# The S5 parameters prepared anew: fused on VectorE, padded on ScalarE, loaded by GpSimd, and the S5 scans joined

## The chip, the cores and the metric

One core of one Trainium2 chip runs the whole kernel. The number reported is device time in microseconds of that core, as the median of several runs. The engines are TensorE (PE; its weight loads are PEld), VectorE (DVE), ScalarE (ACT), GpSimd (POOL) and SyncE (SP, which here only issues DMAs). Each engine takes its instructions in the order in which they were written for it, and waits at an instruction until everything that it depends on is there.

## The reference

Two layers of three sublayers each on 256 tokens of width 1024, all in float32. Each sublayer ends in `h = LN(alpha h + f(h))`.

```
sublayer 0, 2, 3, 5:  f = 0.5 * (silu(h W_gate) * (h W_up)) W_out        # width 2816
sublayer 1 (S5):      u = h W_in                                         # 64 groups of 16 channels, 64 complex states each
    dt = exp(log_dt); lam = exp(a dt)         # a = a_re + i a_im
    Bbar = (lam - 1) / a * B
    state[t] = lam state[t-1] + Bbar u[t]     # forward scan over 256 tokens
    y = gelu(Re(C state) + d u);  f = (y * sigmoid(y W_glu + b)) W_out
sublayer 4 (gMLP):    u, v = split(gelu(h W_in + b)); v = LN(v)
    f = (u * (mask(W_s) v + b_s)) W_out       # token mixing in blocks of 128
```

## The kernel before, in words

**Precision.** Matmuls run in float32r. Each operand is split into two parts, `hi` (the rounded value) and `lo` (the rest), and each product is three matmuls: hi hi, hi lo, lo hi.

**Weights.** `Stream` holds all weights as blocks of 1 MiB in the order of their use. SP loads a block into one of three buffers (`raw`), ACT casts it to `hi` (L82), DVE subtracts to get `lo` (L83). At most five split blocks exist at a time, those in use counted; this is the ring. `tick()` (L116) is called after every piece of PE's work: it splits one more block if the ring has room and then runs one entry of `ws.background`, a list of work that has nothing to do with the sublayer that is running.

**The first FFN (sublayer 0).** Its width is cut into 11 chunks of 256 columns. `chunk_in(c)` multiplies a chunk for all tokens in two halves m, each a gate part and an up part, and `act_t` (L364) makes silu(gate) * up on ACT and DVE and writes it, split again, into a buffer `gt` (seven exist). Its order is silu (ACT), product `sgg` (DVE), cast `gt` (ACT), difference `gt` (DVE). Beside chunk c the output product of chunk c - 2 runs in two steps, `step_out(c - 2, 0)` and `(…, 1)`, one for each half of the tokens. So chunk 0 has 3 ticks, chunk 1 has 4 and each later chunk 6 (chunk 10 has no output steps and 4 ticks). `close` does the last three output blocks, and the norm of each half of the tokens, and starts the next sublayer's transposes (`make_xt`, L177).

**The preparation.** `prepare_s5` (L577) turns the S5 parameters into the layouts of their use while the first FFN runs. Its pieces are entries of `ws.background`. A hand-written table (L878 to L907) gives each tick one piece for POOL (`work_p`) and pieces for DVE and ACT (`work_v`):

- `exp`, `angle`, `sines`, `lambdas`, `coefs`: dt, lam, lam^4 and the coefficients of Bbar. Everything is 128 x 32 (state x pair of groups), real and imaginary parts in tiles of their own, on POOL. `spread` copies the coefficients into another layout (16 copies, POOL).
- `seed`, `base_table`, `table`: cosines and sines of k times the angle of lam^4, grown by doubling; one `table` for each of eight groups of 128 channels (`ct`), two levels each, on POOL. Every second `table` writes into a buffer of the tag `gt`.
- `b_rows` and `b_turn`: Bbar lam^d in rows, transposed on DVE, written to DRAM (`rows`) by SP.
- `c_load`, `c_turn`, `c_lam`: C is loaded into a cleared tile where the two groups of a pair stand apart (half of it zeros), transposed, and multiplied by lam three times: once on DVE, twice on POOL.
- `b_bar` and `k_products`: short products K on PE. They need Bbar and C lam^d, zero where the groups differ (`bar`, `c`); `k_products(0)` and `(2)` stand at entries 58 and 59 of the table.

The results go to DRAM (`rows`, `tc`, `res["k"]`) and come back in the S5 sublayer. All loads of the preparation are issued by SP, between those of the weights.

**The S5 loop (`s5`, L910).** For each of eight `ct`: `inject` (PE), `turned` (DVE, two instructions: times cosines and sines), `sums` (POOL, two), `scan` (DVE, eight scans over 64 steps: two parts x four pairs), `turned` and `sums` again, `read_out` (PE), `activate` (DVE, ACT), `split_y` (POOL). Between them DVE splits the weights of the gate and PE multiplies with them.

Of the kernel before, what the change touches and what calls it, by code (L numbers as in the profile page):

```python
# [38 lines left out]
N_SMALL = 18  # L39


class Stream:
# [94 lines left out]
def hybrid(ctx: ExitStack, tc: tile.TileContext, a: dict, out: bass.AP, subs=SUBS):  # L137
# [137 lines left out]
    def plan_ffn(li, fi, fine):  # L275
# [31 lines left out]
    def ffn(ids, li, si, first, last):  # L307
# [132 lines left out]
    def close_mixer(ids, li, si, operand, gb, hscale, eps, last):  # L440
        """The output product of a mixer; operand(k, t): the two parts of 128 of its columns, transposed."""
# [18 lines left out]
    def load_gmlp(pool):  # L460
        """The parameters of the gMLP mixer but for its two projections; W_s masked and transposed."""
# [24 lines left out]
    def gmlp(plan, par, pool, li, si, first, last):  # L486
# [20 lines left out]
        def step_u(hd):  # L507
            """u of one head, its channels on the partitions."""
# [19 lines left out]
        def spatial(hd):  # L528
            """The token mixing of two heads and the gate, in place of u."""
# [35 lines left out]
    def load_column(pool, src, name):  # L565
        """[1024] as [128, 8], channel 128 j + p at [p, j]."""
# [10 lines left out]
    def prepare_s5(sm, qp, dram):  # L577
        """Parameters of the S5 mixer in the layouts of its use, as pieces of work for the time of the first FFN.

        State s of pair q is state s % 64 of group 2 q + s // 64. Four tokens make one step:  # L580
        S' = lam^4 S + sum over t of lam^(3-t) B u[4k+t], y[4k+3] = Re(C S'), and for t < 3
        y[4k+t] = Re(C lam^(t+1) S) + sum over i <= t of K(t-i) u[4k+i], K(d) = Re(C lam^d B).
        With lam^4 = m e^(i phi), e^(-i phi k) S is a scan with real factors m.
        """
        V, G = nc.vector, nc.gpsimd
        MUL, ADD, SUB = ALU.mult, ALU.add, ALU.subtract
        small = lambda name: sm.tile([P, PAIRS], F32, tag="sm", name=name, bufs=N_SMALL)
# [3 lines left out]
        def tt(e, o, x, y, op):  # L591
            e.tensor_tensor(o, x, y, op=op)  # L592
# [6 lines left out]
        load = nc.sync.dma_start  # L599
        m4 = sm.tile([P, PAIRS], F32, name="m4")  # L600
        val, zs = {}, []
        res = {"m4": m4, "rows": dram.tile([CT, P, 2, 4, P], F32, name="rows"), "tc": dram.tile([CT, P, D], F32, name="tc")}

        def loads():
            x = val["raw"] = big("s5a", [PAIRS, 4, P])
            for j, nm in enumerate(("s5_a_re", "s5_a_im")):
                load(out=x[:, j], in_=a[nm][0].rearrange("(q g) p -> q (g p)", g=2))
            val["dt2"] = sm.tile([PAIRS, 2], F32, name="dt2")
            load(out=val["dt2"], in_=a["s5_log_dt"][0].rearrange("(q g) -> q g", g=2))
            for j, nm in enumerate(("s5_d", "s5_b_glu")):  # L610
                load(out=x[CT * j:CT * j + CT, 3], in_=a[nm][0].rearrange("(j p) -> j p", p=P))

        def exp(x, name):
            """e^x: 2^k of the nearest integer k to x / ln 2, in two factors, times a polynomial in the rest."""
            k, r, o = small("ek"), small("er"), small(name)
            e = [small("ee") for _ in range(2)]
            ts(G, x, x, -170.0, ALU.max, 170.0, ALU.min)
            ts(G, k, x, 1.0 / math.log(2.0), MUL, ROUND, ADD)
            ts(G, k, k, -ROUND, ADD, 1.0, MUL)
            ts(G, r, k, -LN2[0], MUL, 0.0, ADD)  # L620
            tt(G, r, x, r, ADD)
            ts(G, o, k, -LN2[1], MUL, 0.0, ADD)
            tt(G, r, r, o, ADD)
            ts(G, o, r, 1.0 / 5040.0, MUL, 1.0 / 720.0, ADD)
            for n in (120.0, 24.0, 6.0, 2.0, 1.0, 1.0):
                tt(G, o, o, r, MUL)
                ts(G, o, o, 1.0 / n, ADD, 1.0, MUL)
            ts(G, r, k, -126.0, ALU.max, 127.0, ALU.min)
            tt(G, k, k, r, SUB)
            for j, part in enumerate((r, k)):  # L630
                ts(G, e[j], part, 127.0, ADD, ROUND, ADD)
            val[name], val["e"] = o, e

        def exp_end(name):
            for e in val["e"]:
                V.tensor_scalar(e.bitcast(I32), e.bitcast(I32), 23, None, op0=ALU.logical_shift_left)
                tt(G, val[name], val[name], e, MUL)

        def turn_a():
            x = val["raw"]  # L640
            G.tensor_copy(x[:, 2].rearrange("q (g p) -> q g p", g=2), over(val["dt2"], 64))
# [4 lines left out]
            for j, nm in enumerate(("ar", "ai", "ldt")):  # L646
                val[nm] = small(nm)
                nc.scalar.copy(val[nm], ps[:, PAIRS * j:PAIRS * j + PAIRS])
            dg = sm.tile([P, 2 * CT], F32, name="dg")
            res["d"], res["bg"] = dg[:, 0:CT], dg[:, CT:2 * CT]  # L650
            nc.scalar.copy(dg, ps[:, 3 * PAIRS:3 * PAIRS + 2 * CT])
            exp(val["ldt"], "dt")

        def angle():
            exp_end("dt")
            th, n, x = tt(G, small("th"), val["ai"], val["dt"], MUL), small("n"), small("x")
            ts(G, n, th, 1.0 / (2.0 * math.pi), MUL, ROUND, ADD)
            ts(G, n, n, -ROUND, ADD, 1.0, MUL)
            for part in TWO_PI:
                ts(G, x, n, -part, MUL, 0.0, ADD)  # L660
                tt(G, th, th, x, ADD)
            ts(G, th, th, 3.1415925, ALU.min, -3.1415925, ALU.max)
            val["th"] = th

        def magnitude():
            exp(tt(G, small("adr"), val["ar"], val["dt"], MUL), "mag")

        def sines():
            cs, sn = small("cs"), small("sn")
            nc.scalar.activation(cs, val["th"], AF.Sin, scale=0.5)  # L670
            nc.scalar.activation(sn, val["th"], AF.Sin)
            val["cs"], val["sn"] = cs, sn
            exp_end("mag")

        def lambdas():
            cs, sn, mag, ar, ai = (val[x] for x in ("cs", "sn", "mag", "ar", "ai"))
            tt(G, cs, cs, cs, MUL)
            ts(G, cs, cs, -2.0, MUL, 1.0, ADD)
            lr, li, den, t1 = small("lr"), small("li"), small("den"), small("t1")
            tt(G, m4, mag, mag, MUL)  # L680
            tt(G, m4, m4, m4, MUL)
            tt(G, lr, mag, cs, MUL)
            tt(G, li, mag, sn, MUL)
            tt(G, den, ar, ar, MUL)
            tt(G, t1, ai, ai, MUL)
            tt(G, den, den, t1, ADD)
            val.update(lr=lr, li=li, den=den)
# [513 lines left out]
```

## Time and profile before

| | |
|---|---|
| runs | 1043.42, 1044.12, 1046.18 us; median 1044.12 |
| profiled execution | span 1044.0 us, the only time that it has |
| busy, share of the span | PE 92%, DVE 62%, ACT 40%, POOL 29% |
| mean granted clock of TensorE | 0.964 |
| DMA | 194.86 MB, mean 187 GB/s |

A row of the timeline has its start and duration in us, the engine, line and operation, `out<-in`, the shape, and in brackets the idle time before it with what ended it. A row of groups has a count, the busy time, and the mean duration in ns. A row of windows has PE, PEld, DVE, ACT and POOL busy time in the stretch, PE's granted clock, the DMA engines' busy share and GB/s. The row of a source line has minimum, median and maximum in ns.

### The profile page before, as it was taken

The numbers are of one execution on the slowest core, as the hardware profiler recorded it, in microseconds if no ns is written. First come the engines' busy times: TensorE is split into PE (matmuls) and PEld (weight loads), VectorE is DVE, ScalarE is ACT, GpSimd is POOL, SyncE is SP. The second block draws the span as 40 slices with busy tenths as digits, with TensorE's granted clock in tenths as the row PEclk, the third lists the DMA queues.
The fourth block names the chain that finished last, engine by engine and source line by source line (L and its number), as shares of the span: only waits on it lengthen the run. The fifth ranks groups of instructions, "written<-read, shape, count | busy, mean of one in ns | idle before, by whom it ended". The sixth has DMA issues, their size and how long they took to land.

```text
span 1044.0 us, 16750 instructions
## 1 busy us (share of the span) xinstructions
PE 964.5 (92%) x6988; PEld 871.9 (84%) x6988; DVE 651.6 (62%) x726; ACT 413.1 (40%) x467; POOL 302.0 (29%) x461
## 2 busy tenths in 40 slices
PE   7999974577988889999999999999999999999996
PEld 6999963475877678999999799999978979999995
DVE  5659834588489776654536764545388785545444
ACT  5462333232143244453533363534335535443430
POOL 1589999998156421000000400000031030000001
PEclk9999996697998999999999999999999999999999
DMA  9977553385466434746455667465544565546431
GB/s 282 205 216 236 184 150 126 130 298 180 169 216 239 149 127 161 258 147 216 164 200 178 223 209 258 149 215 170 193 162 174 190 209 194 204 160 221 142 122 41
DMA packets 146124, 194.86 MB, mean 187 GB/s; under 512 B 26992, under 2 KB 117184, under 8 KB 146048
## 3 DMA queue, kind: packets, MB, share of 16 engines
q1 hardware_dynamic: 142304, 180.81, 52.7%
q0 software_dynamic: 3456, 12.45, 3.5%
q8 instruction: 55, 0.90, 0.3%
q10 hardware_dynamic: 288, 0.52, 0.1%
q14 instruction: 21, 0.17, 0.0%
HBM read 183.94 MB, written 9.83 MB: 186 GB/s over the span
## 4 chain that ended last, share of the span: by engine, by line
PE 59%; POOL 20%; DVE 10%; issue 4%; ACT 3%; DMA 2%; SPq 1%; POOLq 0%; DVEq 0%; ACTq 0%
PE ips L192 10%; PE ips L191 10%; PE ips L190 10%; PE acc L183 5%; PE acc L184 5%; PE acc L185 5%; POOL rot L972 3%; DVE lo L83 2%; POOL fac L592 2%; POOL t L592 2%; PE ips L185 2%; POOL cl L592 2%; PE ips L183 2%; PE ips L184 2%; POOL tb L592 2%
## 5 line engine op out<-in xcount | busy, mean ns | idle before, releaser
L83 DVE TENSOR_TENSOR lo<-raw,hi 128x2048 fp32r<-128x2048 f32 (+1 forms) x146 | 333.9, 2318 | 85.2 <-ACT hi L82 82.5
L190 PE MATMUL ips<-xt,hi 128*128 128x256 f32 x1184 | 335.3, 283 | 0.0
L191 PE MATMUL ips<-xt,hi 128*128 128x256 f32 x1184 | 335.0, 283 | 0.0
L192 PE MATMUL ips<-xt,lo 128*128 128x256 f32 x1184 | 335.0, 283 | 0.0
L82 ACT CAST hi<-raw 128x2048 fp32r<-128x2048 f32 (+1 forms) x156 | 275.1, 1797 | 62.7 <-PE acc L185 22.1
L190 PEld LDWEIGHTS ips<-xt,hi 128*128 128x128 f32 x1184 | 227.1, 192 | 1.4
L191 PEld LDWEIGHTS ips<-xt,hi 128*128 128x128 f32 x1184 | 227.2, 192 | 1.4
L192 PEld LDWEIGHTS ips<-xt,lo 128*128 128x128 f32 x1184 | 227.1, 192 | 0.0
L203 POOL TENSOR_SCALAR rstd<-mv 128x1 f32<-128x1 f32 x14 | 10.3, 733 | 586.3 <-DVE mv L224 564.4
L183 PE MATMUL acc<-hi,gt 128*128 128x512 f32 x352 | 141.9, 403 | 29.3 <-ACT hi L82 29.3
L184 PE MATMUL acc<-lo,gt 128*128 128x512 f32 x352 | 141.2, 401 | 4.6 <-DVE lo L83 4.6
L185 PE MATMUL acc<-hi,gt 128*128 128x512 f32 x352 | 140.2, 398 | 0.0
L369 DVE TENSOR_TENSOR sgg<-ips,sgg 128x256 f32<-128x256 f32 x74 | 31.1, 420 | 158.8 <-ACT sgg L368 158.8
L368 ACT ACTIVATE sgg<-ips 128x256 f32<-128x256 f32 x74 | 28.4, 383 | 207.9 <-PE ips L192 204.0
L183 PEld LDWEIGHTS acc<-hi,gt 128*128 128x128 f32 x352 | 68.5, 195 | 43.2 <-ACT hi L82 29.7
L370 ACT CAST gt<-sgg 128x256 fp32r<-128x256 f32 x74 | 30.1, 406 | 149.9 <-DVE sgg L369 100.9
L184 PEld LDWEIGHTS acc<-lo,gt 128*128 128x128 f32 x352 | 68.3, 194 | 18.8 <-DVE lo L83 5.9
L185 PEld LDWEIGHTS acc<-hi,gt 128*128 128x128 f32 x352 | 68.1, 193 | 14.7
L371 DVE TENSOR_TENSOR gt<-sgg,gt 128x256 fp32r<-128x256 f32 x74 | 34.1, 461 | 69.9 <-ACT gt L370 69.9
L183 PE MATMUL ips<-hi,xt 128*128 128x512 f32 x112 | 45.9, 410 | 1.7 <-ACT hi L92 1.0
L972 POOL TENSOR_TENSOR rot<-rot 128x256 f32<-128x256 f32 x32 | 35.8, 1137 | 40.1 <-DVE rot L966 39.8
L185 PE MATMUL ips<-hi,xt 128*128 128x512 f32 x112 | 45.0, 402 | 0.1
(250 smaller groups left out, 1275.9 us busy)
## 6 DMA issues: line engine op xcount, KB each, us to landing
raw<-in_ffn_w_in SPq DMA_DIRECT2D x172, 512.0 KB, 5.5
raw<-in_ffn_w_out SPq DMA_DIRECT2D x44, 1024.0 KB, 5.1
raw<-in_g_w_in SPq DMA_DIRECT2D x8, 1024.0 KB, 5.9
rows<-w SPq DMA_DIRECT2D x8, 512.0 KB, 6.0
raw<-in_s_w_in SPq DMA_DIRECT2D x4, 1024.0 KB, 5.5
raw<-in_s_w_glu SPq DMA_DIRECT2D x4, 1024.0 KB, 5.0
w<-rows SPq DMA_DIRECT2D x8, 512.0 KB, 5.8
tc<-tc SPq DMA_DIRECT2D x8, 512.0 KB, 5.1
```

The lines of the kernel that those rows point to most:

```text
L82: nc.scalar.copy(hi[:, s], raw[:, s])
L83: eng[p % len(eng)].tensor_tensor(lo[:, s], raw[:, s], hi[:, s].bitcast(F32), op=ALU.subtract)
L183: nc.tensor.matmul(ps, xh, wh, start=start, stop=False)
L184: nc.tensor.matmul(ps, xh, wl, start=False, stop=False)
L185: nc.tensor.matmul(ps, xl, wh, start=False, stop=stop)
L190: nc.tensor.matmul(ps, wh, xh, start=start, stop=False)
L191: nc.tensor.matmul(ps, wh, xl, start=False, stop=False)
L192: nc.tensor.matmul(ps, wl, xh, start=False, stop=stop)
L369: nc.vector.tensor_tensor(g, ps[:, 1], sg, op=ALU.mult)
L371: nc.vector.tensor_tensor(x[:, 1], g, x[:, 0].bitcast(F32), op=ALU.subtract)
L592: e.tensor_tensor(o, x, y, op=op)
L972: G.tensor_tensor(dst[:, j], x, z, op=ops[j])
```

## The change

`prepare_s5` is written anew, and `s5` gets new scans. The other functions are unchanged but for their docstrings and for `load_ln`, which in the first FFN now goes through POOL as in the others.

- Real and imaginary parts lie in one tile (128 x 2 x 32), and complex operations are fused: `exp` is 18 instructions (scalar_tensor_tensor), `angle` 7, `lambdas` 10, `coefs` 25, all on DVE. `seed` and `base_table` stay on POOL. `spread` goes to ACT.
- `table` goes to DVE, for two `ct` at a time, in buffers of the preparation's own; a copy of the base on ACT comes first.
- C and B are kept compact (16 columns for each pair, not 32 with zeros). `product` makes one complex part in three DVE instructions on 128 x 512, and `pad` spreads the result into the zero-padded tile with two ACT copies of 64 x 512. `c_lam` for powers 2 and 3 is made from C directly with lam^2 and lam^3, in two tiles `cl` that both powers use.
- All DMAs of the preparation are issued by POOL (60 in all), and the tiles are cleared by POOL.
- The table of entries is replaced by one list with costs. Each tick adds 1.3 us of credit (at most 1.95 is kept), and runs pieces from the head of the list while the credit is above zero or the piece costs nothing; a piece also has a first tick.
- `scan` runs over four pairs at once: the factors lie in a tile `fm` of 128 x 4 x 64, zero at the first step of each pair, filled by ACT (`factors`).

```diff
-                gb = load_ln(li, si, nc.sync if first else nc.gpsimd)
+                gb = load_ln(li, si, nc.gpsimd)
 ...
+        def cmul(o, x, y):
+            p, q = both("p"), both("q")
+            tt(p, x, twice(y[:, 0]), MUL)
+            tt(q, x, twice(y[:, 1]), MUL)
+            tt(o[:, 0], p[:, 0], q[:, 1], SUB)
+            tt(o[:, 1], p[:, 1], q[:, 0], ADD)
 ...
+        def spread(t):
+            for sq in range(4):
+                A.copy(val["cq"][32 * t:32 * t + 32, :, :, sq], val["cf"][t][32 * sq:32 * sq + 32])
 ...
+        def table(r, level):
+            q = slice(8 * r, 8 * r + 8)
             if level == 4:
-                if ct % 2:
-                    val["tb"] = gt_p.tile([P, 2, 4, NS], F32, tag="gt", name="tb")
+                val["tb"] = big("tb", [P, 2, 8, NS])
+                A.copy(val["tb"][:, :, :, 0:16], val["base"][:, :, q])
+            L, z, tb = 1 << level, val["zs"][level + 2], val["tb"]
+            x = ln_p.tile([P, 2, 2, 8, 32], F32, tag="r", name="tx", bufs=2)[:, :, :, :, 0:L]
+            for j in range(2):
+                tt(x[:, j], tb[:, :, :, 0:L], twice(over(z[:, j, q], L)), MUL)
+            tt(tb[:, 0, :, L:2 * L], x[:, 0, 0], x[:, 1, 1], SUB)
+            tt(tb[:, 1, :, L:2 * L], x[:, 0, 1], x[:, 1, 0], ADD)
 ...
+        def pad(dst, src):
             for g in range(2):
                 s = slice(64 * g, 64 * g + 64)
+                A.copy(dst[s, :, g], src[s])
+
+        def product(j, x, y, dst, signs):
+            pq = big("pq", [P, 2, PAIRS, 16])
+            tt(pq[:, 0], x[:, j], over(y[:, 0], 16), MUL)
+            tt(pq[:, 1], x[:, 1 - j], over(y[:, 1], 16), MUL)
+            tt(pq[:, 0], pq[:, 0], pq[:, 1], signs[j])
+            pad(dst, pq[:, 0])
 ...
+        def c_turn():
+            cc = val["cc"] = big("cc", [P, 2, PAIRS, 16])
+            V.transpose(cc.rearrange("p j q c -> p (j q c)"), val["cz"].rearrange("p j r c -> p (j r c)"))
+            A.mul(cc[:, 1], cc[:, 1], -1.0)
+            for j in range(2):
+                pad(val["c", 0, j], cc[:, j])
 ...
+        add(4, 0.1, turn_a)
+        add(5, 2.4, lambda: exp(val["ldt"], "dt"))
+        add(6, 1.0, angle)
+        add(7, 2.4, lambda: exp(val["ad"][:, 0], "mag"))
+        add(8, 1.3, c_turn)
+        add(9, 1.3, lambdas)
+        add(10, 0, seed, 0)
+        add(10, 3.0, coefs)
+        for t in range(T):
+            add(11, 0, spread, t)
+        for i, (f, *args) in enumerate([(b_bar, 0), (b_bar, 1), (c_lam, 1, 0), (c_lam, 1, 1), (k_products, 0), (c_lam, 2, 0),
+                                        (c_lam, 2, 1), (k_products, 2), (c_lam, 3, 0), (c_lam, 3, 1)]):
+            add(12, 0 if f is k_products else 1.8, f, *args)
+            if i < 6:
+                add(12, 0, seed, i + 1)
+        for level in range(4):
+            add(20 + level, 0, base_table, level)
 ...
+        for r in range(4):
+            for level in (4, 5):
+                add(25, (1.1, 1.9)[level - 4], table, r, level)
 ...
+        for part in range(4):
+            for j in range(2):
+                add(30, 1.9, b_rows, j, part)
+                add(30, 1.3, b_turn, j, part)
 ...
+        def tick():
+            credit[0] = min(credit[0] + PREP_US, 1.5 * PREP_US)
+            while work and work[0][0] <= ticks[0] and (credit[0] > 0.0 or work[0][1] == 0):
+                _, cost, f = work.pop(0)
+                credit[0] -= cost
+                f()
+            ticks[0] += 1
+            if work:
+                ws.background.insert(0, tick)
 ...
+        def factors(ct):
+            m = res["m4"][:, 4 * ct:4 * ct + 4].unsqueeze(2).broadcast_to([P, 4, NS - 1])
+            nc.scalar.copy(fm[ct % 2][:, :, 1:NS], m)
 ...
         def scan(ct):
+            f = fm[ct % 2].rearrange("p q k -> p (q k)")
             for j in range(2):
-                for q in range(4):
-                    f = res["m4"][:, 4 * ct + q:4 * ct + q + 1].broadcast_to([P, NS])
-                    V.tensor_tensor_scan(buf["s"][:, j, q], f, buf["v"][:, j, q], 0.0, op0=MUL, op1=ADD)
+                x, z = (buf[n][:, j].rearrange("p q k -> p (q k)") for n in "sv")
+                V.tensor_tensor_scan(x, f, z, 0.0, op0=MUL, op1=ADD)
```

More of the change, by code (lines that the diff above doesn't have):

```diff
@@ L645, in turn_a @@
             nc.tensor.transpose(ps[:, 3 * PAIRS:3 * PAIRS + 2 * CT], x[:2 * CT, 3], ident[:2 * CT, :2 * CT])
-            for j, nm in enumerate(("ar", "ai", "ldt")):
-                val[nm] = small(nm)
-                nc.scalar.copy(val[nm], ps[:, PAIRS * j:PAIRS * j + PAIRS])
+            ch = big("ch", [P, 16, 2, PAIRS])
+            val.update(aa=ch[:, 0], ad=ch[:, 1], lam=[None, ch[:, 3], ch[:, 4], ch[:, 5]], l1=ch[:, 6],
+                       zs=[ch[:, 2]] + [ch[:, 9 + i] for i in range(7)])
@@ L662, in angle @@
[L662 to L673, printed above, removed]
-        def lambdas():
[L676 to L687, printed above, removed]
@@ L741, in grow @@
[L741 to L755 removed]
+                stt(th, n, -part, MUL, th, ADD)
@@ new lines, in coefs @@
+        def coefs():
+            aa, lam, l1 = val["aa"], val["lam"], val["l1"]
+            fac = big("fac", [P, 2 * T, 2, PAIRS])
+            cf = val["cf"] = [fac[:, t] for t in range(T)]
+            val["cq"] = fac[:, T:2 * T].rearrange("p a b c -> p (a b c)").rearrange("p (r j s) -> p r j s", r=2, s=4)
+            p, q = both("p"), both("q")
+            tt(p, l1, twice(aa[:, 0]), MUL)
+            tt(q, l1, twice(aa[:, 1]), MUL)
+            c = cf[T - 1]
+            tt(c[:, 0], p[:, 0], q[:, 1], ADD)
+            tt(c[:, 1], p[:, 1], q[:, 0], SUB)
+            tt(c, c, twice(val["den"]), MUL)
+            for t in reversed(range(T - 1)):
+                cmul(cf[t], cf[t + 1], lam[1])
+            for d in (2, 3):
+                cmul(lam[d], lam[d - 1], lam[1])
@@ L816, in b_load @@
                 G.memset(x, 0.0)
[L818 to L821 removed]
+                G.memset(val["bar"][j], 0.0)
+        def pad(dst, src):
             for g in range(2):
                 s = slice(64 * g, 64 * g + 64)
[L824 removed]
+                A.copy(dst[s, :, g], src[s])
@@ new lines, in c_turn, with c_lam @@
+        def c_turn():
[4 more added lines that the diff above has]
+                pad(val["c", 0, j], cc[:, j])
+        def c_lam(d, j):
+            if d > 1 and j == 0:
+                if d == 2:
+                    val["cl"] = [big("cl", [P, PAIRS, 2, 16]) for _ in range(2)]
+                    for x in val["cl"]:
+                        G.memset(x, 0.0)
+                val["c", d, 0], val["c", d, 1] = val["cl"]
+            product(j, val["cc"], val["lam"][d], val["c", d, j], (ADD, SUB))
+            if d > 1:
+                s = 512 + 256 * (d - 2) + 128 * j
+                G.dma_start(out=res["tc"][:, :, s:s + 128].rearrange("t p x -> p t x"),
+                            in_=val["c", d, j].rearrange("p (t q) g c -> p t (q g c)", t=CT))
@@ L871, in k_products @@
-            nc.scalar.copy(val["k"][:, :, d:d + n], ps)
+                                         c[:, :, 4 * ct + q], start=j == 0, stop=j == 1, tile_position=(0, 32 * q))
+            A.copy(val["k"][:, :, d:d + n], ps)
             if d:
-                nc.gpsimd.dma_start(out=res["k"], in_=val["k"].rearrange("p t d c -> p (t d c)"))
-        def call(f, *args):
-            return lambda: f(*args)
-        none = lambda: None
-        work_p = [loads] + [none] * 4 + [turn_a] + [none] * 3 + [angle, magnitude] + [none] * 3 + [sines, lambdas, none, coefs, spread]
@@ L880, in prepare_s5 @@
-        work_p += [seed] * 7 + [call(base_table, l) for l in range(4)]
-        work_p += [call(table, ct, l) for ct in range(CT) for l in range(4, 6)]
-        work_p += [none] * 4 + [call(c_lam, d, j, part, G) for d in (2, 3) for j in range(2) for part in range(3)]
-        work_v = {}
-        def place(at, step, *items):
-            for i, x in enumerate(items):
-                work_v.setdefault(at + i * step, []).append(x)
-        copies = lambda half: [call(copy_b, j, half, n) for j in range(2) for n in (32, 64)]
@@ L890, in prepare_s5 @@
-        rows = lambda part: [call(f, j, part) for j in range(2) for f in (b_rows, b_turn)]
-        place(2, 1, *[call(c_load, j) for j in range(2)])
-        place(4, 1, b_load, *[call(load_b, j, 0) for j in range(2)])
-        place(9, 1, *[call(c_turn, j) for j in range(2)])
-        place(11, 1, *copies(0))
-        place(18, 1, *[call(c_lam, 1, j, part, V) for j in range(2) for part in range(3)])
-        place(24, 1, call(b_bar, 0), call(b_bar, 1))
-        place(27, 1, *rows(0), *rows(1))
@@ new lines, in prepare_s5, with add @@
+        work = []
+        def add(first, cost, f, *args):
+            work.append((first, cost, lambda: f(*args)))
+        add(0, 0, loads)
+        add(1, 0, c_load, 0)
+        add(2, 0, c_load, 1)
+        add(2, 0, pads)
+        add(3, 0, b_load)
+        add(4, 0.1, turn_a)
[5 more added lines that the diff above has]
+        add(10, 0, seed, 0)
@@ L908, in prepare_s5 @@
+        credit, ticks = [0.0], [0]
+        def tick():
[7 more added lines that the diff above has]
+                ws.background.insert(0, tick)
+        ws.background.append(tick)
         return res
@@ L917, in s5 @@
         tcs = [qp.tile([P, D], F32, tag="q", name="tc") for _ in range(2)] + [ln_p.tile([P, D], F32, tag="gam", name="tc")]
+        fm = [res["sm"].tile([P, 4, NS], F32, tag="fm", name="fm", bufs=2) for _ in range(2)]
+        for x in fm:
+            G.memset(x[:, :, 0:1], 0.0)
         buf, pend = {}, []
```

298 lines of the change are left out of this document (129 added, 169 removed).

## The prediction

> **What bounds the kernel now.** I read the page first: the busy shares, the 40 slices (26 us each) and the chain.
>
> ```profile
> PE 964.5 (92%) x6988; PEld 871.9 (84%) x6988; DVE 651.6 (62%) x726; ACT 413.1 (40%) x467; POOL 302.0 (29%) x461
> ...
> PE   7999974577988889999999999999999999999996
> ...
> POOL 1589999998156421000000400000031030000001
> ...
> PEclk9999996697998999999999999999999999999999
> ...
> PE 59%; POOL 20%; DVE 10%; issue 4%; ACT 3%; DMA 2%; SPq 1%; POOLq 0%; DVEq 0%; ACTq 0%
> ```
>
> Over the whole span TensorE is the engine that sets the time (92%), but not in slices 6 to 10 (130 to 260 us). There PE falls to 4 to 7 tenths while POOL is at 8 or 9, and the chain of work that ended last runs over POOL for 20% of the span, 209 us. So the preparation on POOL bounds the first FFN. The windows show where PE stands:
>
> ```profile
> 150.00:160.00 10.00, 1.18 (x10) 0.97 (x9) 0.00 (x0) 0.00 (x0) 9.15 (x23) 0.77 0.00 0
> ...
> 160.00:170.00 10.00, 0.00 (x0) 0.00 (x0) 0.51 (x1) 2.17 (x2) 9.14 (x29) 0.50 0.14 52
> ...
> 190.00:200.00 10.00, 1.10 (x10) 0.90 (x8) 0.30 (x1) 0.74 (x2) 8.86 (x29) 0.65 0.14 53
> ...
> 230.00:240.00 10.00, 5.18 (x128) 4.45 (x129) 8.06 (x7) 5.55 (x7) 9.60 (x5) 0.70 1.02 361
> ...
> 250.00:260.00 10.00, 2.90 (x12) 2.00 (x11) 9.53 (x6) 0.81 (x2) 8.90 (x6) 0.72 0.10 37
> ```
>
> The first number after the stretch is PE's busy time, and the clock stands behind the five engines. PE waits 8.8, 10.0, 8.9, 4.8 and 7.1 us in these five stretches alone, and POOL is busy in all of them. The list of waits names the first three:
>
> ```profile
> ACT gt L370 <- POOL s5t L592: 39.5, 2, 24.8
> ```
>
> ACT waits twice, 24.8 us at the longest, to write `gt`: `table` has taken buffers of that tag and POOL fills them late.
>
> How long would the stage take without waits? From PE's timeline:
>
> ```profile
> 23.57 0.28 PE L190 MATMUL ips<-xt,hi 128*128 128x256 f32 x1
> ...
> 26.44 0.28 PE L190 MATMUL ips<-xt,hi 128*128 128x256 f32 x1
> ...
> 136.10 0.39 PE L183 MATMUL acc<-hi,gt 128*128 128x512 f32 x1
> ...
> 138.82 0.39 PE L183 MATMUL acc<-hi,gt 128*128 128x512 f32 x1
> ...
> 258.62 1.12 PE L169 MATMUL tps<-ident,h 128*128 128x128 f32 x4 [1.64 <-DVE h L213]
> ```
>
> 24 matmuls of the input product lie between the first two rows, 0.1196 us each, and 12 of the output product between the next two, 0.227 us each. A chunk is 96 and 24 of them: 11.5 + 5.4 = 16.9 us. From 23.6, where chunk 1 begins: 11.5 + 8 x 16.9 + 11.5 + 8.2 (first half of the close) = 190, and 8 more to the end of the transposes that open the next sublayer: 198. They end at 258.62 + 1.12 = 259.7, so the first FFN loses 62 us. That is what the change can win, and the S5 loop behind it a little.
>
> **The change, part by part.** Its sum is made against the profiled execution: its span is 1044.0 us, the median of the runs 1044.12, and I add nothing between them.
>
> *What goes away.* All 62 us, as waits for POOL: no `gt` buffer is lent to `table`, C lam^2 and C lam^3 leave POOL. What comes instead is work for DVE and ACT, in the program's order, between the weights' splits. The prices:
>
> ```profile
> L592 DVE TENSOR_TENSOR prod<-b,fac 128x512 f32<-128x512 f32 x4 | 2.7, 714 | 0.0
> ...
> L592 DVE TENSOR_TENSOR s<-prod 128x256 f32<-128x256 f32 x16 | 6.9, 473 | 0.3
> ...
> L805 DVE STREAM_TRANSPOSE w<-s 128x1024 f32<-128x1024 f32 x8 | 9.9, 1235 | 0.0
> ...
> L636 DVE TENSOR_SCALAR ee<-ee 128x32 int32<-128x32 int32 x4 | 0.6, 177 | 0.8 <-POOL ee L596 0.8
> ...
> L369 DVE TENSOR_TENSOR sgg<-ips,sgg 128x256 f32<-128x256 f32 x20 | 8.2, 411 | 4.3 <-ACT sgg L368 4.3
> ...
> L82 ACT CAST hi<-raw 128x2048 fp32r<-128x2048 f32 x33 | 61.6, 1902 | 13.2 <-DMA raw<-in_ffn_w_in 11.4 <-DMA raw<-in_ffn_w_out 1.1 <-DMA raw<-in_s_w_in 0.8
> ...
> L871 ACT COPY k<-kps 128x512 f32<-128x512 f32 x1 | 0.6, 577 | 0.0
> ...
> L648 ACT COPY ldt<-aps 128x32 f32<-128x32 f32 x1 | 0.2, 219 | 0.0
> ```
>
> A DVE instruction on 128x32 takes 0.18, with the gap to a dependent one I take 0.2. A product of 512 columns takes 0.71, a transpose 1.24, an ACT copy 0.58 (512 columns) or 0.22 (32), the cast `hi` 1.90.
>
> *Up to K.* `k_products(0)` is issued in the same tick as the last product it needs, and PE takes its instructions in order. Which tick follows from the budget: the items from `exp` to the third product cost 2.4+1+2.4+1.3+1.3+3+5.4 = 16.8, the credit is 1.95 at tick 5 and grows by 1.3, so the fourth product starts in tick 17. With 3 ticks in chunk 0, 4 in chunk 1 and 6 in each chunk after, that is behind the first output step of chunk 3. PE is there at 23.6 + 11.5 + 16.9 + 11.5 + 2.7 = 66. DVE has by then to do: ten splits; six activations; 53 small instructions (two `exp` of 18, `angle` 7, `lambdas` 10); one transpose; 25 in `coefs`; four products of three. What a split and an activation cost, and how far DVE may lag:
>
> ```profile
> 87.69 0.46 DVE L371 TENSOR_TENSOR gt<-sgg,gt 128x256 fp32r<-128x256 f32 x1 [0.47 <-ACT gt L370]
> ...
> 109.73 0.43 DVE L371 TENSOR_TENSOR gt<-sgg,gt 128x256 fp32r<-128x256 f32 x1 [0.47 <-ACT gt L370]
> ...
> 111.54 2.29 DVE L83 TENSOR_TENSOR lo<-raw,hi 128x2048 fp32r<-128x2048 f32 x1 [1.39 <-ACT hi L82]
> ...
> 130.00 0.43 DVE L371 TENSOR_TENSOR gt<-sgg,gt 128x256 fp32r<-128x256 f32 x1 [0.47 <-ACT gt L370]
> ...
> 134.16 0.50 PE L184 MATMUL acc<-lo,gt 128*128 128x512 f32 x1 [1.31 <-DVE lo L83]
> ```
>
> A split is 2.29, and 1.39 of waiting for the cast before it; an activation 0.41 + 0.47 + 0.43 = 1.31. So 22.9 + 7.9 + 10.6 + 1.2 + 5.0 + 8.6 = 56.2 of work and 13.9 of waiting for casts. ACT now stands in the same line: its pads wait for DVE's product and the next cast stands behind them. That adds 5 copies of `c_turn` (2.9), 16 of `spread` (3.5) and 4 pairs of pads (4.6), less 2 that run beside `lambdas`: 9. From 23.6 that gives 103, so PE waits 103 - 66 = 37 us where it waited for nothing before. From below: were ACT's share wholly covered, 28; from above: every small instruction at 0.25, 41. I take 37.
>
> The second K (tick 20) waits again: two products, two pairs of pads, three splits, an activation and casts make 21 us after the first, against 2.0 + 2.7 + 5.7 and the cold clock on PE: 7 us. The two K cost 3.8 themselves, as before, and each long wait leaves PE at half rate:
>
> ```profile
> 170.09 0.80 PE L183 MATMUL acc<-hi,gt 128*128 128x512 f32 x1 [18.91 <-ACT hi L82]
> ...
> 176.00 0.39 PE L183 MATMUL acc<-hi,gt 128*128 128x512 f32 x1
> ...
> 234.81 1.83 PE L869 MATMUL kps<-cl,bar 128*32 128x32 f32 x120 [5.86 <-POOL cl L592]
> ```
>
> A matmul takes 0.80 after the wait of 18.9 and 0.39 only 6 us later: 3 us lost a time, 5.6 for both. The third row is K's price, 1.83, and its wait of 5.86 now.
>
> *From there to the close.* The timeline of DVE quoted above has the ends of chunks 4, 5 and 6 as DVE works through them: 22.0 and 20.3 us apart, with some 11 and 10.3 us of preparation in each, so 10 to 11 us are the FFN's own. The new budget gives six ticks x 1.3 = 7.8 a chunk; `b_rows` and `b_turn`, budgeted at 3.2, take 2 x 0.71 + 2 x 0.47 + 1.24 less overlap, 3.4: so 8.3. That is 18.3 to 19.3 a chunk; I take 19, 2.1 over PE's 16.9, 10.5 in five chunks. The ring of split weights hides some: before, PE first waited for a split at 134.16 (1.31 us), when DVE had lost 5.1 + 3.4 in two chunks. I let it hide 9. Then `table` waits on ACT for `base_table`, which stands on POOL behind the last DMA of C lam^3:
>
> ```profile
> 144.66 0.27 POOL L592 TENSOR_TENSOR base<-base,zc 128x32 f32<-128x32 f32 x1
> ...
> 153.91 0.72 POOL L592 TENSOR_TENSOR base<-base,s5t 128x256 f32<-128x256 f32 x1
> ...
> L596 POOL TENSOR_SCALAR dt<-dt x6: 216/216/2136, 41.6 to 48.7; 128x32 f32<-128x32 f32 x6
> ...
> L856 POOL DMA_DIRECT2D tc<-cl x4: 926/948/977, 224.7 to 258.3; - x4
> ```
>
> 24 instructions from 144.66 to 154.63 are 10 us, with DVE idle beside them. So 10.5 + 10 - 9 = 11.5 (0 to 25). At the close DVE still has its backlog when the norm is due; the wait there was 7.1, without POOL's big instructions but with the backlog I take 6 (0 to 9).
>
> *DMAs.* They leave SP, where they stood between the weights, for POOL, where little stands before them: the 16 loads of C need no clear by DVE any more and meet the very first weights.
>
> ```profile
> 17.12 1.91 ACT L82 CAST hi<-raw 128x2048 fp32r<-128x2048 f32 x1 [1.79 <-DMA raw<-in_ffn_w_in]
> ...
> cz<-in_s_c_re SPq DMA_DIRECT2D x4, 64.0 KB, 6.1
> ```
>
> The split of block 2 already waited 1.79 us for its DMA. C is eight times 64 KB; I take 2 us of delay (0, if the engines have room, to 5). The 60 issues on POOL cost up to 0.98 each (row of L856), 59 us, beside other work. The 2.2 us that POOL's small instructions sometimes take (216 to 2136 ns in the row of L596) beside a DVE split do not appear in its DMA rows, 926 to 977. [...]
>
> *S5 loop.*
>
> ```profile
> 313.24 2.09 DVE L978 TENSOR_TENSOR_SCAN rot<-m,rot 128x64 f32<-128x64 f32 x8 [0.62 <-POOL rot L972]
> ...
> 321.61 2.08 DVE L978 TENSOR_TENSOR_SCAN rot<-m,rot 128x64 f32<-128x64 f32 x8 [0.62 <-POOL rot L972]
> ```
>
> A tile takes 8.37 us, and the chain runs DVE scan, turn, POOL sums, split, sums. Eight scans take 2.09. Two of 256: between 0.41 each (an ordinary instruction of that size) and four times 0.26; 64 columns at 0.26 over a fixed 0.11 give 2.3 ns a column, 0.68. That saves 0.7 a tile on the chain, 6 us in eight (0.5 to 10). `factors` on ACT is covered by ACT's idle time; uncovered it would cost 8 x 0.36.
>
> *Sum.* The first FFN: 198 + 3.8 + 37 + 5.6 + 7 + 11.5 + 6 = 268.9 against 259.7, +9; start +2; S5 -6. 1044 + 5 = 1049.
>
> **The rivals.** First, faster: after the second K everything is synchronous again and DVE keeps up, because the 10 us of `base_table` find the ring full and 8.3 us a chunk fit. For it: 18.3 a chunk would be 7 in five, less than the ring's 9. Against: the base wait comes first and uses the ring up. It would take away 17.5: 1031. It decides from a DVE pace of 18.7 a chunk without the base wait. Second, no change: the small instructions overlap (0.13 apart where independent), which puts K five us earlier, and the sums cancel: 1044. Third, POOL late: every second of the 24 instructions of `base_table` and the DMAs ahead waits out a split, 12 x 1.2 = 14 more: 1063. For it the row of L596; against it that DVE is idle then.
>
> **How the numbers follow.** My forecast 0.40 at 1049 (own range 1042 to 1058); the first rival 0.27; no change 0.17; POOL late 0.13; 0.03 for still faster, if K hardly waits. About 0.3%, 3 us, is what a measurement of this kernel can tell. So faster 0.30, same 0.17, slower 0.53. The range goes from 1024 (first rival with the S5 loop's full 10 and no start cost) to 1066 (POOL late, and no gain from the scans).
>
> **What will show it.** A PE wait of 30 us or more before the first K, for ACT's pad, at about 66 to 103 us; a second one of some 7; no ACT wait for `gt` from POOL; ACT waiting for `base` around tick 25; scans of about 0.7; a tile in 7.6 us. A first K that waits under 15 us makes the prediction wrong on the fast side, POOL busy from 100 to 230 on the slow side.

## The result and the profile after

| | median us | runs | against the kernel before |
|---|---|---|---|
| before | 1045.15 | 1043.42 to 1047.8 | |
| after | 1056.86 | 1056.07 to 1059.57 | 1.0118 [1.0095, 1.0141] |

The change makes the kernel slower by about 12 us; the forecast was 1049, 5 us slower, so the side was right and the size less than half. The row of before has one run more than the table above (1047.8). The profiled execution has a span of 1054.2 us, 10.2 more than that of before. The same views as before, from the page of after:

```profile
PE 961.9 (91%) x6988; PEld 870.8 (83%) x6988; DVE 655.5 (62%) x788; ACT 436.0 (41%) x517; POOL 186.7 (18%) x255
...
PE   7790598999799899999999999999999999999996
...
POOL 8043135221326612000000400000021030000001
...
PEclk9895699999898999999999999999999999999998
...
PE 55%; DVE 17%; POOL 6%; issue 5%; ACT 4%; POOLq 0%; DVEq 0%; ACTq 0%
```

POOL has fallen from 29% to 18% and from 20% of the chain to 6%: what the change does to GpSimd, it does. But the hole in PE's line has only moved. It was in slices 6 to 10; now it is in slices 4 and 5 (79 to 132 us), and the chain runs over VectorE for 17% instead of 10%. PE's own timeline after, the waits of the first FFN:

```profile
25.10 0.39 PE L192 MATMUL ips<-xt,lo 128*128 128x256 f32 x1 [1.82 <-DVE lo L83]
28.41 0.39 PE L192 MATMUL ips<-xt,lo 128*128 128x256 f32 x1 [1.61 <-DVE lo L83]
38.11 0.31 PE L636 MATMUL aps<-ident,s5a 32*128 32x32 f32 x1 [4.68 <-ACT s5a L633]
...
103.00 0.44 PE L868 MATMUL kps<-cm,bar 128*32 128x64 f32 x8 [24.80 <-ACT cm L816]
110.46 3.43 PE L868 MATMUL kps<-cm,bar 128*32 128x64 f32 x120 [7.02 <-ACT cm L816]
...
125.50 0.27 PE L868 MATMUL kps<-cl,bar 128*32 128x32 f32 x8 [1.99 <-ACT cl L816]
130.70 1.83 PE L868 MATMUL kps<-cl,bar 128*32 128x32 f32 x120 [4.92 <-POOL ch L596]
...
185.33 0.39 PE L192 MATMUL ips<-xt,lo 128*128 128x256 f32 x1 [1.70 <-DVE lo L83]
...
274.05 1.97 PE L169 MATMUL tps<-ident,h 128*128 128x128 f32 x8 [5.51 <-DVE h L213]
```

Two K products wait 24.80 + 7.02 and 1.99 + 4.92 us for ScalarE's pads (the last row names a seed on POOL, the last to report; ScalarE's pad of the same product ends just then). The last transposes of the stage end at 274.05 + 1.97 = 276.0, against 259.7 before: 16.3 us lost in the first FFN. The span grew by 10.2, so the rest won 6.1.

What stands behind the first wait is seen in VectorE's timeline after, and it is more than lateness:

```profile
108.34 0.69 DVE L596 TENSOR_TENSOR pq<-pq 128x512 f32<-128x512 f32 x1
119.80 2.29 DVE L83 TENSOR_TENSOR lo<-raw,hi 128x2048 fp32r<-128x2048 f32 x1 [10.77 <-ACT hi L82]
...
140.62 0.42 DVE L369 TENSOR_TENSOR sgg<-ips,sgg 128x256 f32<-128x256 f32 x1 [8.01 <-ACT sgg L368]
```

While PE stands at K, no split block is used up, the ring is full, and ScalarE's next cast and next silu wait for PE (3.33 us of ScalarE's wait at 117.86 and 5.96 at 140.20 end with a matmul); so VectorE, the late engine, idles 10.8 and 8.0 us itself.

### The profile page after: what moved, and what is told of

Read it like the earlier page. It is cut to its first block, busy times and chain, and to the rows that moved or that the text cites. A ratio compares the mean times of both kernels' runs of the same rounds, so it can differ in the third digit from the quotient of the medians.

```text
span 1054.2 us, 16638 instructions
## 1 busy us (share of the span) xinstructions
PE 961.9 (91%) x6988; PEld 870.8 (83%) x6988; DVE 655.5 (62%) x788; ACT 436.0 (41%) x517; POOL 186.7 (18%) x255
## 4 chain that ended last, share of the span: by engine, by line
PE 55%; DVE 17%; POOL 6%; issue 5%; ACT 4%; POOLq 0%; DVEq 0%; ACTq 0%
PE ips L192 10%; PE ips L191 10%; PE ips L190 10%; PE acc L183 5%; PE acc L184 5%; PE acc L185 5%; DVE lo L83 5%; POOL rot L1010 3%; ACT hi L82 2%; DVE h L213 2%; DVE rot L1016 1%; DVE bst L222 1%; PE ips L185 1%; DVE r L221 1%; PE ips L183 1%
## 5 line engine op out<-in xcount | busy, mean ns | idle before, releaser
L83 DVE TENSOR_TENSOR lo<-raw,hi 128x2048 fp32r<-128x2048 f32 (+1 forms) x146 | 325.6, 2261 | 107.1 <-ACT hi L82 107.1
L184 PE MATMUL acc<-lo,gt 128*128 128x512 f32 x352 | 139.0, 395 | 4.7 <-DVE lo L83 4.7
L183 PE MATMUL acc<-hi,gt 128*128 128x512 f32 x352 | 139.4, 396 | 1.1 <-ACT gt L370 1.1
L185 PE MATMUL acc<-hi,gt 128*128 128x512 f32 x352 | 138.0, 392 | 0.0
L183 PEld LDWEIGHTS acc<-hi,gt 128*128 128x128 f32 x352 | 66.9, 190 | 14.7 <-ACT gt L370 1.8
L185 PEld LDWEIGHTS acc<-hi,gt 128*128 128x128 f32 x352 | 66.7, 190 | 14.4 <-DVE gt L371 0.3
L371 DVE TENSOR_TENSOR gt<-sgg,gt 128x256 fp32r<-128x256 f32 x74 | 31.6, 427 | 35.1 <-ACT gt L370 35.1
L184 PE MATMUL ips<-lo,xt 128*128 128x512 f32 x112 | 44.5, 398 | 0.0
```

The source lines that it names most:

```text
L83: eng[p % len(eng)].tensor_tensor(lo[:, s], raw[:, s], hi[:, s].bitcast(F32), op=ALU.subtract)
L183: nc.tensor.matmul(ps, xh, wh, start=start, stop=False)
L184: nc.tensor.matmul(ps, xh, wl, start=False, stop=False)
L185: nc.tensor.matmul(ps, xl, wh, start=False, stop=stop)
L371: nc.vector.tensor_tensor(x[:, 1], g, x[:, 0].bitcast(F32), op=ALU.subtract)
```

## The experiments

Two theories. **A (the line):** the preparation on VectorE and ScalarE, an in-order line with the weights' splits, is what is late; K's wait shows the lateness and adds VectorE's idle time. **B (the position):** the waits are the price of where K stands in PE's order, and go away with it. Ratios are to the kernel before, run beside each, with a 95% interval in brackets.

**K's waits taken away.** Two ways: K's matmuls at their place, of operands that are ready early (the values of K change), and K's matmuls unchanged but issued later, with `base_table` put ahead of them.

```
# e5_k_ready, in k_products:  c = C's first part;  lhsT = C's first part instead of bar
# e1_k_late:  b_bar x2, c_lam 1 x2, c_lam 2 x2, base_table;  tick 24: k_products 0, 2;  then c_lam 3 x2
```

> The changed kernel with the K products at their old place but of operands that are ready since c_turn (both sides the first part of C): their matmuls stay, their wait for the products goes; K's values are others. Theory A (lag): TensorE goes on and meets split weights that are late, since VectorE and ScalarE still do all the preparation in the same order; only the 10.8 and 8.0 us in which they stood still behind TensorE, and some 3 to 5 us of cold clock, are won: 1032 (1026 to 1040), with new waits for lo of 15 us or more. Theory B (position): 1054 - 38.7 - 4 = 1011 (1005 to 1018), with no new waits of more than 5 us together.

> The changed kernel with the two K products issued together in tick 24 (end of chunk 4) instead of ticks 17 and 20; C lam^3 after them, base_table ahead. Theory A (lag): VectorE and ScalarE together are late by their own serial chain; the wait at K only shows it, and costs beside it what VectorE then idles because the ring of split weights is full behind a standing TensorE (10.8 us from 109 to 120 and 8.0 us from 132.6 to 140.6). Moved, the two waits (31.8 and 6.9 us) come down to 15 to 25 us, part of it as waits for split weights: 1054 less 12 to 19, about 1039 (1034 to 1046). Theory B (position): the waits are the price of the place of K in TensorE's order and go with it: 1054 - 38.7 - some 3 of cold clock = 1012 (1008 to 1022).

Measured: with ready operands 1045.89 us, 1.0013 [1.0000, 1.0026]; with K moved 1043.38, 0.9993 [0.9981, 1.0006]. So of the 38.7 us of waits only 11 and 13 are won (by the ratios). Theory B falls. A foretold K moved within its range, but was 14 us too hopeful for the ready operands (1032 expected): it had left `base_table` out, which is 7.3 us of them. With K moved, its products still wait 13.9 us at their later place, which is the line's lateness and not the place. PE's timeline with ready operands shows where the rest went:

```profile
94.31 0.58 PE L190 MATMUL ips<-xt,hi 128*128 128x256 f32 x1 [3.65 <-DVE sgg L369]
...
129.37 0.80 PE L183 MATMUL acc<-hi,gt 128*128 128x512 f32 x1 [4.81 <-ACT hi L82]
...
158.88 0.80 PE L183 MATMUL acc<-hi,gt 128*128 128x512 f32 x1 [7.30 <-ACT hi L82]
```

Nine waits of PE between 80 and 172 us, these the longest, still sum to 24.2 us there. The last, 7.30, is that for `base_table`, which the prediction had put on the path. In the changed kernel PE does not wait then; our reading, not tested by itself, is that PE's stop at K had let the ring fill. ScalarE's timeline, after and with ready operands:

```profile
165.15 0.41 ACT L753 COPY tb<-base 128x256 f32<-128x256 f32 x1 [12.51 <-POOL base L596]
```

```profile
151.12 0.41 ACT L753 COPY tb<-base 128x256 f32<-128x256 f32 x1 [12.47 <-POOL base L596]
```

The same 12.5 us: in the one PE's next wait comes at 175 us (0.92), in the other at once (7.30).

**ScalarE taken out of the line.** First the pads and `spread` on GpSimd; then, as that was taken back, each product written by VectorE straight into its padded tile and `spread` put off.

```
# e2_pads_pool, in pad and spread:  A.copy(...) -> G.tensor_copy(...)
# e6_direct, in product:
-  tt(pq[:, 0], pq[:, 0], pq[:, 1], signs[j]);  pad(dst, pq[:, 0])
+  for g in range(2):  s = slice(64 * g, 64 * g + 64);  tt(dst[s, :, g], pq[s, 0], pq[s, 1], signs[j])
#   and spread at tick 24 instead of 11
```

> The changed kernel with the pads and the 16 copies of spread on GpSimd instead of ScalarE (c_turn's sign stays on ScalarE). Theory A with ScalarE in the line, as the prediction had it: VectorE's waits for the cast behind a pad or behind spread (3.29 at 83.6, 1.4 to 3.2 at each product) go, 8 to 11 us of the first K's wait: 1044 (1040 to 1048). Rival C (VectorE alone): its 56 us of work set the place of K and ScalarE's copies lie beside it: 1054, within 2. Rival D (GpSimd late): its copies stand behind the seeds' 8 instructions each, some of 2.3 us beside a VectorE instruction, and the first K waits as long or longer: 1056 to 1064.

> The changed kernel, each product of B bar and C lam^d written by VectorE straight into its padded tile (two sums on 64 partitions in place of one and of ScalarE's two copies), and spread moved from tick 11 to tick 24. Where the pads were put on GpSimd, VectorE had finished C lam at 100.6 instead of 109.0, though it began 2.7 us later, but spread's 16 copies (11.4 us on GpSimd) and the seeds held the pads back to 108. Theory A (ScalarE in the line): with neither behind it, VectorE finishes at about 101 and K stands right behind: the K waits fall by 7 to 11 us together, 1057 - 9 = 1048 (1044 to 1051). Rival C (VectorE's own work alone): 8 more instructions of 0.69 us are 5.5 us more, 1058 to 1062.

Measured: on GpSimd 1053.24, 1.0083 [1.0053, 1.0113], where 1044 was expected; written directly 1045.48, 1.0012 [0.9999, 1.0026]. The first number alone speaks for rival C. The timelines do not. With the pads on GpSimd, VectorE, GpSimd and PE:

```profile
99.64 0.98 DVE L596 TENSOR_TENSOR pq<-pq 128x512 f32<-128x512 f32 x1
```

```profile
77.48 11.41 POOL L715 COPY fac<-fac 32x64 f32<-32x64 f32 x16 [5.28 <-DVE fac L596]
...
106.82 1.27 POOL L816 COPY cm<-pq 64x512 f32<-64x512 f32 x2
```

```profile
108.14 0.44 PE L868 MATMUL kps<-cm,bar 128*32 128x64 f32 x8 [3.40 <-POOL cm L816]
```

VectorE has the last operand at 100.6, 8.4 us earlier than the 109.0 after; but GpSimd spends 11.4 us on `spread` (5.0 on ScalarE), has a seed ahead of each pair of pads, and pads this operand only at 106.8 to 108.1. So the gain was there and GpSimd took it back: rival D in part, not C. Written directly, K is free of both. PE's timeline (the view ends at 103, so the second row counts only the matmuls up to there):

```profile
97.62 0.44 PE L869 MATMUL kps<-cm,bar 128*32 128x64 f32 x8 [19.65 <-DVE cm L596]
102.57 0.71 PE L869 MATMUL kps<-cm,bar 128*32 128x64 f32 x17 [4.51 <-DVE cm L596]
```

The wait is 24.2 instead of 31.8 and ends 7.9 us earlier, though VectorE does more work. The 11 us won are A's 9, within the stated 1044 to 1051. So ScalarE's pads and `spread` in the line cost 8 to 11 us together here; how they share it was not measured. The 24 us that stay belong to VectorE's line: from 23.6 to 102.4 us it is busy 60.5 and waits some 16 for ScalarE's weight casts and activations.

**The start.** C's loads later, and the copy of log dt from ScalarE to GpSimd; then each alone (B's loads later too).

```
# e3_start:       c_load at ticks 4, 5 (b_load thereby at 2);  s5a's copy on GpSimd at tick 3
# e9_loads_late:  c_load at ticks 4, 5;  b_load at 6
# e10_early_copy: s5a's copy on GpSimd at tick 3
```

> The changed kernel with the loads of C at ticks 4 and 5 instead of 1 and 2, and the spreading of log dt on GpSimd at tick 3 instead of on ScalarE in tick 4. In the changed kernel TensorE waits 1.82 and 1.61 us for late weights at 23 to 28 us and 4.68 for that copy. Theory A (the line of VectorE decides when K can start): TensorE comes to K earlier and waits there longer; only what makes VectorE later, the 3.4 us of weights, is won: 1053.5 (1051 to 1055). Theory B (the waits add up): all 8.1 us: 1048.7 (1046 to 1051).

> The changed kernel with the loads of C at ticks 4 and 5 (not 1 and 2) and those of B at tick 6 (not 3); the copy of log dt stays. Where only C was moved, B's loads of 64-byte rows came a tick earlier into the start and the split at 23.6 us waited 8.3 us for its weights. Theory A (VectorE's line sets K): the 3.4 us of late weights made VectorE itself late, so they are won once: 1057 - 3.4 = 1053.5 (1051 to 1055.5). Theory B' (the loads collide wherever they stand): 1057 or more.

> The changed kernel with the spreading of log dt on GpSimd at tick 3; TensorE's wait of 4.68 us for that copy on ScalarE at 38 us goes, all else stays. Theory A: VectorE's line isn't touched, TensorE comes 4.7 us earlier to the first K and waits there 4.7 us longer: no change, 1057 within 2. Theory B (waits add up): 1052.3 (1050 to 1054).

Measured: 1058.22 (1.0126 [1.0106, 1.0147]), 1056.31 (1.0120 [1.0104, 1.0135]), 1056.67 (1.0120 [1.0104, 1.0136]). The copy alone is the cleanest test of A against B: PE's 4.68 us wait at 38 us is gone, and nothing is won, as A expected. PE's timeline there:

```profile
71.30 0.50 PE L183 MATMUL acc<-hi,gt 128*128 128x512 f32 x1 [1.05 <-ACT hi L82]
...
103.31 0.44 PE L870 MATMUL kps<-cm,bar 128*32 128x64 f32 x8 [25.30 <-ACT cm L818]
110.76 3.43 PE L870 MATMUL kps<-cm,bar 128*32 128x64 f32 x120 [7.01 <-ACT cm L818]
```

K's second group starts at 110.76, after at 110.46: the wait ahead of it is merely handed on, though not all to K. PE now waits 2.9 us for split weights at 71 to 74 (1.05, the row above, and 1.83), the next eight matmuls take 0.61 to 0.72 us where those of after from 75.3 on take 0.39 or 0.40, and K waits 0.5 longer. Moving the loads won nothing clear in either run: 1058.22 and 1056.31, where A had 1053.5; the second lies between A's range and the 1057 of B'. GpSimd's timelines show why (C's first, then both later):

```profile
13.57 3.36 POOL L839 DMA_DIRECT2D cz<-in_s_c_re  x6
```

```profile
9.50 4.52 POOL L837 DMA_DIRECT2D cz<-in_s_c_re  x8
```

A tick is a place in the program, not a time. GpSimd had little else to do then and issued the loads of ticks 4 and 5 at 13.6 and 9.5 us, when PE had not begun its second chunk. They still met the first weights: between 20 and 280 us ScalarE's casts waited 10.7 us (8.3 the longest) and 5.8 us for the FFN's input weights, 6.2 after. What it would be worth to have the loads later was not measured.

**The scans.** Undone in the changed kernel, and done alone in the kernel before (with one buffer of factors, copied just ahead).

```
# e4_eight_scans, after's scan(ct):  for j, q: tensor_tensor_scan(s[:, j, q], m4 broadcast, v[:, j, q]); no factors
# e12_scans_only, before's scan(ct): factors(ct);  for j: tensor_tensor_scan(s[:, j], fm, v[:, j])
```

> The changed kernel with the eight scans of 64 columns per tile instead of two of 256, and without the copies of the factors. Theory S1: the scan lies on the chain of a tile, and a tile goes from 8.09 back to 8.37 us: 8 x 0.28 = 2.2 slower, 1056.5 against 1054.2. Theory S2 (the prediction's term): all 6 us that the part after the first FFN gained come from the scans: 1060. Theory S3: the scans are hidden and nothing changes: 1054.

> The kernel before with one thing of the change alone: two scans of 256 columns a tile instead of eight of 64, the factors copied on ScalarE (one buffer, copied just ahead of the scans). Undoing it in the changed kernel cost 2 to 4 us. Theory S1 (a tile 8.37 to 8.09 us, and a little at the last one): 1044.1 - 2 to 4.5 = 1041 (1039.5 to 1042.5). Theory S2 (all of the 6 us): 1038. Rival: the copy of the factors stands ahead of the scan, one buffer, and takes the gain back: 1044.

Measured: undone 1060.0, 1.0157 [1.0124, 1.0190], 3 to 4 us slower than after, though this interval overlaps that of after; alone 1040.25, 0.9955 [0.9937, 0.9972], 4.3 us faster than before. The expectations for the undone scans were reckoned from the span, 1054.2, and 1060 is what S2 has there. From the median, 1056.9, S1 gives 1059, S2 1063 and S3 1057, and 1060 lies nearest to S1. The second run is the clearer one: S1 has 1041, S2 1038, the rival 1044. From the end of the first FFN's transposes to the end of the span it is 784.3 us before, 780.6 with the scans alone, 778.2 after and 782.5 after with eight scans: the scans are worth 3.7 to 4.3 of the 6.1 (the traced run with eight scans was the longest of its four, 1064.98). So S1 is borne out: a tile takes 8.08 instead of 8.37 wherever the scans are joined. About half of the gain is the last tile, 8.78 before, 6.67 after and 6.68 with the scans alone; why it gains so much was not tested. The other 2 us of S5 were not traced to one step.

**Together.** Three forms, each mending what the trace of the last one showed.

```
# e7_combo:  e6_direct + e3_start; all seeds right behind coefs, base_table between the first four products; both K in tick 23
# e8_combo2: base_table behind C lam^2; b_load at tick 6
# e11_combo3: C lam^2's tiles cleared right behind b_bar, base_table behind that, ahead of C lam
```

> All remedies together in the changed kernel: later loads of C and the earlier copy, products written straight into padded tiles, spread in tick 24, all seeds and base_table directly behind lambdas (GpSimd is idle there), both K in tick 23. Theory A: the remedies act on one line and add: 13 (K moved, as measured) + 3.4 (start) + 8 (ScalarE out of the line) + up to 10 (VectorE's wait for base_table, 10.2 us): 1057 - 33 = 1024 (1014 to 1034). Rival: VectorE has more work than TensorE's pace leaves room for (86 us of preparation against 6.4 free us a chunk), and it settles near the kernel with K moved: 1036 to 1043.

> All remedies together once more, with two mends that its trace asks for: base_table behind C lam^2 instead of between the products (there GpSimd came late to the clearing of C lam^2's tiles, and VectorE stood 7.95 us for it before the second K), and the loads of B at tick 6, C at 4 and 5. Theory A: 1030.4 - 8 - 3 = 1019.5 (1015 to 1025). Rival (VectorE has too much work; what is won at K comes back as waits for split weights by the close): 1028 to 1031.

> All remedies, third form: C lam^2's tiles are cleared right behind b_bar, and base_table stands behind that, ahead of C lam. In the form before, the wait of 8 us at the second K had only moved: VectorE stood 10.3 us for base_table at 126 to 136, and TensorE then waited 8 us for split weights between 152 and 223. Theory A (waits of the line, one by one): with GpSimd early for both, neither is left: 1028.5 - 6 to 10 = 1020.5 (1017 to 1024). Rival (too much work on VectorE): the split weights are late all the same: 1027 to 1030.

Measured: 1030.37 (0.9858 [0.9844, 0.9873]), 1028.52 (0.9854 [0.9836, 0.9872]), 1024.69 (0.9810 [0.9793, 0.9828]). The first lies within A's range, 6 us short of its 1024; the second is the rival's number. VectorE's timeline, first form, then second:

```profile
115.58 1.39 DVE L596 TENSOR_TENSOR cl<-pq 64x512 f32<-64x512 f32 x2 [7.95 <-POOL cl L854]
```

```profile
136.18 0.76 DVE L596 TENSOR_TENSOR tx<-tb,ch 128x256 f32<-128x256 f32 x2 [10.30 <-ACT tb L755]
```

In the second form the expected 8 us went nearly whole into another wait, as its rival said: GpSimd has the clearing of C lam^2's tiles and `base_table` to do, and VectorE waits for whichever is second. The third form gives GpSimd both early, and PE's timeline has left:

```profile
101.64 3.43 PE L872 MATMUL kps<-cm,bar 128*32 128x64 f32 x120 [4.83 <-DVE cm L596]
106.99 0.33 PE L872 MATMUL kps<-cl,bar 128*32 128x32 f32 x8 [1.92 <-DVE cl L596]
111.92 1.83 PE L872 MATMUL kps<-cl,bar 128*32 128x32 f32 x120 [4.61 <-DVE cl L596]
```

11.4 us at K instead of 38.7. 3.8 us of the step were won where 6 to 10 were expected, between A's range and the rival's. They are PE's waits for split weights behind K, 7.1 us in the second form and 3.5 in the third. A new wait has come up: VectorE stands 3.8 us at 121 to 125 for the store of C lam^2, whose tiles C lam^3 uses again. This is the fastest kernel: 20 us under before and 32 under the change as made.

## Why the prediction was right or wrong

Its frame held: PE stands at K for a line of VectorE and ScalarE, the FFN gets longer, S5 shorter. The size did not: the first FFN +16 for +11 (with the start), S5 -6.1 for -6, so +10 for +5 in the span. By its own steps:

- *Up to K.* Forecast: PE waits 37 us, from 66 to 103, for ScalarE's pad. Measured: 31.8, from 78 to 110. The end came 7 us later and PE itself 12 us later, so that the length lies within the bounds 28 to 41 is partly luck. VectorE's line was too short in the sum: between 23.6 and 109.0 us it is busy 56.3 and idle 29.1, where the sum had 53.4 and 25.7. It makes eleven splits, not ten, and waits 6.8 us for ScalarE's silu ahead of `sgg`, a term that the sum did not have. PE was late by the start (below). That ScalarE stands in the line was put at 9 us; taking it out won 8 to 11.
- *The second K.* Forecast 7, measured 6.9.
- *The clock.* Forecast 5.6 us of half rate behind the waits. An estimate from the windows, PE's busy time times what the granted clock lacks to 1, gives them, and 2.8 us more that was not in the sum (30 to 50 us, clock 0.87 and 0.79, behind the wait at 38):

```profile
30.00:40.00 10.00, 5.32 (x38) 5.00 (x38) 6.05 (x8) 5.10 (x13) 0.00 (x0) 0.87 0.97 272
40.00:50.00 10.00, 10.00 (x70) 10.00 (x70) 6.58 (x22) 3.24 (x4) 0.00 (x0) 0.79 0.61 211
...
100.00:110.00 10.00, 0.44 (x8) 0.23 (x8) 5.73 (x7) 4.05 (x5) 0.95 (x1) 0.50 0.44 144
110.00:120.00 10.00, 9.54 (x152) 8.67 (x153) 0.20 (x1) 2.81 (x3) 0.00 (x0) 0.71 0.19 67
...
120.00:130.00 10.00, 3.79 (x38) 3.50 (x36) 6.89 (x9) 2.71 (x6) 3.71 (x7) 0.80 0.47 157
130.00:140.00 10.00, 9.30 (x168) 9.27 (x169) 1.99 (x3) 2.16 (x4) 2.95 (x5) 0.68 0.38 147
```

  From 110 to 140 that is 2.8 + 0.8 + 3.0 = 6.6 us; K's own matmuls run in it and cost 6.0, against 4.1 before (the sum's 3.8 leaves out a row of 0.27).
- *The start*, the term most mis-sized: 2 us (0 to 5) for DMAs. The late weights cost PE 3.4; what was overlooked is the copy of log dt, 4.7: the change moves it from GpSimd to ScalarE, where it stands behind a weight cast (the excerpt of the diff leaves this line out). That it cost nothing by itself was shown; that it would cost once K were not behind it was not measured alone.
- *The second half.* Forecast 11.5 (0 to 25). Measured: split waits of 8.1 us from 170 on and 1.1 for `gt`, 9.1 together. The steps came as forecast: the wait for `base_table` (12.5 on ScalarE, 10.2 on VectorE) came while PE had split blocks left in the ring; as we read it, PE paid for it in the chunk from 174 to 195, which took 21.3 us where PE alone needs 17.0. The next two chunks took 19.1 and 18.8, and 19 was VectorE's pace in the sum. The close: 5.5 for 6.
- *The scans.* Forecast 0.68 us each and a tile of 7.6; the row of the scan after and the tiles:

```profile
L1016 DVE TENSOR_TENSOR_SCAN rot<-fm,rot x16: 658/930/1212, 305.1 to 361.5; 128x256 f32<-128x256 f32 x16
```

```profile
331.60 0.42 ACT L1042 ACTIVATE y<-y 128x256 f32<-128x256 f32 x1 [5.13 <-DVE y L1041]
339.68 0.42 ACT L1042 ACTIVATE y<-y 128x256 f32<-128x256 f32 x1 [5.11 <-DVE y L1041]
```

  A tile takes 8.08, down by 0.29, not by 0.7. The fixed part of a scan was taken as 0.11 us, which the rows of ordinary instructions give (0.714 for 512 columns, 0.411 for 256); an estimate from the two lengths (0.26 for 64 columns, 0.93 for 256) is 0.04, and so joining saves little: 2 x 0.93 against 8 x 0.26 (1.79 against 2.08 in the timelines, the 0.29 of the tile). So -6 was right as a number by luck: the scans brought some 4 of it, half of that in the last tile.
- *The rivals.* The first (DVE keeps up) did not come: the splits were late after K in spite of a full ring. The second (K five us earlier) did not either: K came 7 us later. Nor did the third (POOL late): of `base_table`'s 24 instructions only two met a split (2.38 and 2.31 us). That such a meeting costs here, and that three DMA issues beside splits were not held up, is seen in POOL's and VectorE's timelines after:

```profile
70.88 2.39 POOL L596 TENSOR_TENSOR ch<-zq 128x32 f32<-128x32 f32 x1
...
202.47 0.72 POOL L795 DMA_DIRECT2D rows<-w  x1 [8.68 <-DVE w L794]
```

```profile
70.86 2.29 DVE L83 TENSOR_TENSOR lo<-raw,hi 128x2048 fp32r<-128x2048 f32 x1 [1.26 <-ACT hi L82]
...
202.10 2.25 DVE L83 TENSOR_TENSOR lo<-raw,hi 128x2048 fp32r<-128x2048 f32 x1
```

  A POOL sum that takes 0.25 us elsewhere starts beside a split, takes 2.39 and ends with it (73.3 and 73.2); a DMA issue beside another split takes its usual 0.72, and two more (217.08 and 256.97) take 0.72 and 0.73. What holds the sum up, no run here shows.

## What to carry to other kernels

An in-order wait hands on what is ahead of it: a stall that is removed in front of a later, longer one wins nothing (4.7 us gone at 38 us, 0 won), and a stall that is removed behind a late line comes back elsewhere (38.7 gone at K, 11 won). So first ask which line is late, and shorten that: here, taking out an engine that only padded between VectorE's product and its next split won some 8 to 11 us. And work on an idle engine goes by the program's order, not by the tick it is listed in (GpSimd issued C's loads of ticks 4 and 5 from 13.6 and 9.5 us on); to place a transfer in time, something that happens at that time would have to stand in front of it (not tried here).

## What the hardware showed beyond the expected

Sixteen copies of 32x64 took 5.0 us on ScalarE and 11.4 on GpSimd, there partly beside two splits; the two pads of 64x512 took 1.25 on ScalarE and, undisturbed, 1.27 on GpSimd. Of two scans of 256 columns that follow each other, one takes 0.66 and the other 1.21 us in the records, 1.8 as a pair; the 0.93 above, the median of the row, lies between the two.
